# Four 32-row blocks in four column tiles: the within-chunk matrices of an S5 layer inside a four-layer decoder trunk

## The chip, the cores and the metric

One core of one Trainium2 chip runs the whole trunk in one launch. The metric is the device time of that launch in microseconds, the median of the runs. Engines are named as the profile names them: PE (TensorE matmul), PEld (its weight load), DVE (VectorE), ACT (ScalarE), POOL (GpSimd), and SP, the queue that issues most DMAs.

## The reference

Four layers on 256 tokens of width 1024, all in float32. Layers 0 and 3 mix tokens with a gated linear recurrence (HGRN2), layer 1 with an mLSTM, layer 2 with a complex diagonal state space (S5); each is followed by a SwiGLU block of hidden width 2816 and by layer norms. The change concerns S5 alone, of whose parameters the kernel makes matrices:

```python
abar = exp((a_re + i*a_im) * dt)                  # 64 groups x 64 states
bbar = (abar - 1) / a * (b_re + i*b_im)           # 64 x 64 x 16 channels
state[t] = abar * state[t-1] + bbar @ u[t]        # per group, complex
y[t] = real(c @ state[t]) + d_skip * u[t]         # c: 64 x 16 x 64
```

The kernel takes four tokens at a time. Inside such a chunk of four, the output at step j + k depends on the input at step j through real(c · abar^k · bbar) with k = 0 to 3, and for k = 0 the skip d is added. These four 16 x 16 matrices per group are the "matrices within a chunk".

## The kernel before

**Layout.** PE works in float32r with every operand split in a high and a low part (`hi`, `lo` of weights, `xh`, `xl` of tokens), so each product is three matmuls (`mm3`, L137, whose matmuls are L140 to L142). In the blocks of the SwiGLU called `across` (L297) the weights are the stationary side and `ws_wide` (L165) issues L170 (512 columns: high and low tokens at once) and L173 (256 columns). Its result stands in a PSUM bank of tag `g`, of which there are two; ACT copies one half out (L304), DVE adds the other (L305), and only then is the bank free for the next but one call of `ws_wide`. ACT casts each weight tile to `hi` (L123), DVE makes `lo` (L124).

**S5's matrices are made early.** `s5_prepare` (L801) returns two lists of small functions, `spans`. They are called one by one from `fill` (L262) between the pieces of the SwiGLU blocks of layer 0 and of layer 1, so their instructions stand among the matmuls of these two stages on every engine; their products go to DRAM and come back in layer 2. `scalars0` to `table_out` make powers of abar and a table; then for each of four quarters q (8 pairs of groups, a pair filling 128 partitions) come `products_b` (L934), `products_bj` (L948), `products_c` (L963), `turn` (L979, PE transposes) and, for e = 0, 1, `within(q, e)` (L990). Temporaries are tiles `t0` (two buffers) and `t1` (one).

**`within` before.** It runs eight times. For each of four pairs x it multiplies the block `bz[..., 3]` (bbar, 128 rows by 32 columns, real and imaginary part in turn) as stationary side with two moving tiles: c itself, 16 columns, from `bc` (L997), and c times three powers, 48 columns, from `cu` (L999). All 16 matmuls write PSUM partitions 0 to 31 of one bank of tag `t`, 64 columns for each x. These are float32 matmuls, which the trace records as two passes each. Then DVE multiplies the bank with `par` (L1003), adds d (L1005), and ACT copies the result three times to lower partitions (L1007); SP stores it (L1008).

**Order.** Each engine executes in order. The order on an engine is set by the tile framework's scheduler from the code and the free buffers, so a changed buffer can move instructions of other lines too.

Of the kernel before, what the change touches and what calls it, by code (L numbers as in the profile page):

```python
# [9 lines left out]
F32 = mybir.dt.float32  # L10
# [4 lines left out]
ALU = mybir.AluOpType  # L15
AX = mybir.AxisListType

P = 128
# [16 lines left out]
class Trunk:  # L35
# [765 lines left out]
    def s5_prepare(self):  # L801


        nc, a = self.nc, self.a
        mk = lambda name, shape: [self.dram.tile(shape, F32, name=f"{name}{b}") for b in range(8)]
        self.s5_b, self.s5_ct, self.s5_cs = mk("s5b", [P, 2, 512]), mk("s5ct", [P, 3, 512]), mk("s5cs", [P, 2, 256])
        c = self.s5const
# [2 lines left out]
        pb = c.tile([P, 2, 3, 32], F32, name="s5pb")  # L810
        co = c.tile([P, 2, 32], F32, name="s5co")
        dd = c.tile([32, 32], F32, name="s5dd")
        par = c.tile([32, 2, 16], F32, name="s5par")
        tt, ts, stt = nc.vector.tensor_tensor, nc.vector.tensor_scalar, nc.vector.scalar_tensor_tensor
        tile_ = lambda tag, shape, **kw: self.s5pool.tile(shape, F32, tag=tag, name=self.uid(tag), **kw)
        k = {}
# [9 lines left out]
        def temps(*shape):  # L826
            n = int(np.prod(shape))
            dims = "abcd"[: len(shape)]
            out = []
            for tag, bufs in (("t0", 2), ("t1", 1)):  # L830
                t = tile_(tag, [P, 1024], bufs=bufs)[:, :n]
                kw = dict(zip(dims, shape))
                out.append(t.rearrange(f"p ({' '.join(dims)}) -> p {' '.join(dims)}", **kw))
            return out

        def squares(x, y):

            t0, t1 = temps(2, pw[:, 0, x, :].shape[1], 32)
            n = t0.shape[2]
            bc = lambda i: pw[:, i, x, :][:, None].broadcast_to([P, 2, n, 32])  # L840
            cmul(pw[:, :, x, :], bc(0), bc(1), t0, t1, pw[:, 0, y, :], pw[:, 1, y, :])
# [47 lines left out]
        def scalars2():  # L889
            squares(slice(0, 5, 4), slice(1, 6, 4))  # L890
            squares(slice(5, 6), slice(6, 7))
            t0, t1 = temps(2, 2, 32)
            bc = lambda i: pw[:, i, 1:2, :][:, None].broadcast_to([P, 2, 2, 32])
            cmul(pw[:, :, 0:2, :], bc(0), bc(1), t0, t1, pw[:, 0, 2:4, :], pw[:, 1, 2:4, :])
            for j in range(3):
                nc.scalar.copy(pb[:, 0, j, :], pw[:, 0, 2 - j, :])
                nc.scalar.mul(pb[:, 1, j, :], pw[:, 1, 2 - j, :], -1.0)
# [10 lines left out]
        def table_double(n):  # L908
            cs, w = k["cs"], k["w"][:, :, 0:16]
            t0, t1 = temps(2, 16, n)  # L910
            bc = lambda i: w[:, i, None, :, None].broadcast_to([P, 2, 16, n])
            cmul(cs[:, :, :, 0:n], bc(0), bc(1), t0, t1, cs[:, 0, :, n : 2 * n], cs[:, 1, :, n : 2 * n])
            if n < 32:
                w2 = tile_("wn", [P, 2, 32], bufs=2)[:, :, 0:16]
                t0, t1 = temps(2, 16)
                bw = lambda i: w[:, i, None, :].broadcast_to([P, 2, 16])
                cmul(w, bw(0), bw(1), t0, t1, w2[:, 0], w2[:, 1])
                k["w"] = w2
# [43 lines left out]

        def products_c(q):  # L963
            f = slice(8 * q, 8 * q + 8)
            cu, t1 = temps(2, 4, 8, 16)
            k["cu"] = cu
            for i in range(2):
                p = lambda r: pw[:, r, 0:4, f][:, :, :, None].broadcast_to([P, 4, 8, 16])
                x = k["bc"][:, 2 + i : 3 + i].broadcast_to([P, 4, 8, 16])
                tt(cu[:, i], x, p(0), ALU.mult)  # L970
                tt(t1[:, i], x, p(1), ALU.mult)
            tt(cu[:, 0], cu[:, 0], t1[:, 1], ALU.subtract)
            tt(cu[:, 1], cu[:, 1], t1[:, 0], ALU.add)
            for i in range(2):
                for g in range(2):
                    r = slice(64 * g, 64 * g + 64)
                    nc.scalar.copy(k["cz"][r, i, :, :, g, :], cu[r, i].rearrange("p j f c -> p f j c"))
# [12 lines left out]
        def within(q, e):  # L990
            b = 2 * q + e
            ps = self.bank("t")
            for x in range(4):
                f, o = 4 * e + x, ps[0:32, x * 64 : (x + 1) * 64]
                w = lambda i: k["bz"][:, i, f, 3].rearrange("p g c -> p (g c)")
                for i in range(2):
                    nc.tensor.matmul(o[:, 0:16], w(i), k["bc"][:, 2 + i, f], start=i == 0, stop=i == 1)  # L997
                for i in range(2):
                    nc.tensor.matmul(o[:, 16:64].rearrange("p (k c) -> p k c", k=3), w(i), k["cu"][:, i, 0:3, f], start=i == 0, stop=i == 1)  # L999
            tm = k["tm"]  # L1000
            dg = tile_("dg", [32, 4, 32])
            tt(dg, self.ident[0:32, None, 0:32].broadcast_to([32, 4, 32]), dd[:, 4 * b : 4 * b + 4, None].broadcast_to([32, 4, 32]), ALU.mult)
            tt(tm[0:32].rearrange("p f (k g c) -> p (f k) g c", g=2, c=16), ps[0:32, 0:256].rearrange("p (n c) -> p n c", c=16)[:, :, None].broadcast_to([32, 16, 2, 16]),  # L1003
               par[:, None].broadcast_to([32, 16, 2, 16]), ALU.mult)
            tt(tm[0:32, :, 0:32], tm[0:32, :, 0:32], dg, ALU.add)  # L1005
            for j in range(1, 4):
                nc.scalar.copy(tm[32 * j : 32 * j + 32, :, 32 * j : P], tm[0:32, :, 0 : P - 32 * j])  # L1007
            nc.sync.dma_start(self.s5_ct[b][:, 2, :], tm.rearrange("p f k -> p (f k)"))  # L1008
# [4 lines left out]
        for s in range(2):  # L1013
            spans[s].append(pads)
            for q in (2 * s, 2 * s + 1):
                spans[s] += [lambda f=f, q=q: f(q) for f in (products_b, products_bj, products_c)]
                for e in range(2):
                    spans[s] += [lambda q=q, e=e, i=i: turn(q, e, i) for i in range(2)] + [lambda q=q, e=e: within(q, e)]
# [250 lines left out]
def consts():  # L1269
    s, c = np.arange(P)[:, None], np.arange(64)[None, :]  # L1270
    lvl = []
    for m in MASKED:
        t = (c // m) * 2 * m + c % m
        same = s // (2 * m) == t // (2 * m)
        lvl.append(np.concatenate([same & ((s // m) % 2 == h) for h in (0, 0, 1, 1)], 1))
    t = np.arange(P)[None, :]
    return {
        "c_ident": np.eye(P, dtype=np.float32),
        "c_par": np.repeat(np.eye(2, dtype=np.float32), 16, 0)[:, :, None].repeat(16, 2),
        "c_lvl": np.stack(lvl, 1).astype(np.float32),  # L1280
        "c_caus": np.where(s > t, np.float32(BIG), np.float32(0.0)),
    }


def layout(i):
# [7 lines left out]
    for g in range(2):  # L1293
# [29 lines left out]
        "w_so": cols_as(so),  # L1323
    })
    out.update(consts())
    return {k: np.ascontiguousarray(v) for k, v in out.items()}

# [13 lines left out]
```

## Time and profile before

| | us |
|---|---|
| runs (3) | 1303.48, 1305.18, 1306.48; median 1305.18 |
| the profiled execution, its own time | 1304.51 |
| its span in the trace | 1302.6 |
| PE busy | 1278.9 (98%) |
| DVE busy | 965.8 (74%) |
| ACT busy | 709.5 (54%) |

The span is cut in the page into 40 slices of 32.6 us with the busy tenths of each engine; the chain of work that ended last is followed back from the last instruction. The calls of `within` start at 252.0, 271.1, 307.1 and 326.2 us (in the SwiGLU block of layer 0) and at 564.1, 583.1, 618.8 and 637.9 us (layer 1). In the timeline, instructions of one line that follow each other are merged: "x4" is four passes, and the second number is from the start of the first to the end of the last.

### The profile page before, as it was taken

What the parts mean: (1) busy time and instruction counts of PE and PEld (TensorE: products, weight loads), DVE (VectorE), ACT (ScalarE), POOL (GpSimd) and SP (SyncE); (2) the same over time, 40 slices, a digit from 0 to 9 for tenths busy, and PEclk for the clock granted to TensorE, in tenths of its full rate; (3) what the DMA queues carried; (4) which work ended last, traced back from release to release, by engine and by line L of the source; (5) the groups of instructions that cost most, each with busy time, mean ns of one, the idle gap of its engine ahead of it and who ended that gap; (6) DMA issues with size and microseconds to landing.
All of it is one profiled execution on the core that took longest, in us unless ns stands there. A gap on an engine that the chain in (4) does not pass through costs nothing.

```text
span 1302.6 us, 18792 instructions
## 1 busy us (share of the span) xinstructions
PE 1278.9 (98%) x7206; PEld 1077.1 (83%) x7206; DVE 965.8 (74%) x1664; ACT 709.5 (54%) x1130; POOL 52.3 (4%) x75
## 2 busy tenths in 40 slices
PE   8999999999999999999998999999999999999997
PEld 6987788888788888888877778888879878888885
DVE  5888789686687699768489877666585886766664
ACT  6755475665466555657442355555458554455550
POOL 0000200000100110000010000000010001000001
PEclk9999999999999999999999999999999999999999
DMA  8833365756374257756567647555555323755540
GB/s 319 289 130 109 127 249 205 258 188 241 117 259 162 97 205 253 237 197 235 183 242 265 237 147 258 178 192 194 194 182 197 134 98 118 267 194 183 182 153 32
DMA packets 46314, 251.00 MB, mean 193 GB/s; under 512 B 5345, under 2 KB 9457, under 8 KB 19857
## 3 DMA queue, kind: packets, MB, share of 16 engines
q1 hardware_dynamic: 45712, 248.08, 53.5%
q0 software_dynamic: 512, 1.73, 0.4%
q8 instruction: 56, 0.92, 0.3%
q14 instruction: 34, 0.27, 0.1%
HBM read 236.16 MB, written 13.63 MB: 192 GB/s over the span
## 4 chain that ended last, share of the span: by engine, by line
PE 91%; DVE 5%; ACT 2%; issue 1%; DMA 1%; POOL 0%; POOLq 0%; SPq 0%; DVEq 0%; ACTq 0%
PE g L170 18%; PE g L140 10%; PE g L142 9%; PE g L141 9%; PE g L173 9%; PE a L140 8%; PE a L141 8%; PE a L142 8%; PE a L594 1%; PE t L1091 1%; DVE lo L124 1%; PE t L225 1%; PE g L1079 1%; DVE att L598 1%; PE t L982 1%
## 5 line engine op out<-in xcount | busy, mean ns | idle before, releaser
L124 DVE TENSOR_TENSOR lo<-w,hi 128x1024 fp32r<-128x1024 f32 (+1 forms) x394 | 476.9, 1219 | 141.2 <-ACT hi L123 132.5
L123 ACT CAST hi<-w 128x1024 fp32r<-128x1024 f32 (+1 forms) x394 | 411.3, 1049 | 191.1 <-PE a L141 110.5
L170 PE MATMUL g<-xx,hi 128*128 128x512 f32 x1024 | 358.3, 395 | 0.0
L173 PE MATMUL g<-xx,lo 128*128 128x256 f32 x1024 | 267.4, 281 | 0.0
L170 PEld LDWEIGHTS g<-xx,hi 128*128 128x128 f32 x1024 | 186.6, 188 | 34.2
L173 PEld LDWEIGHTS g<-xx,lo 128*128 128x128 f32 x1024 | 192.4, 188 | 10.5
L140 PE MATMUL g<-hi,xx 128*128 128x512 f32 x424 | 172.3, 408 | 5.0 <-ACT hi L123 2.4
L141 PE MATMUL g<-hi,xx 128*128 128x512 f32 x424 | 169.8, 401 | 0.0
L142 PE MATMUL g<-lo,xx 128*128 128x512 f32 x424 | 169.2, 401 | 0.0
L140 PE MATMUL a<-hi,hh 128*128 128x512 f32 x344 | 135.8, 397 | 0.0
L141 PE MATMUL a<-hi,hl 128*128 128x512 f32 x344 | 135.7, 395 | 0.0
L142 PE MATMUL a<-lo,hh 128*128 128x512 f32 x344 | 135.4, 394 | 0.0
L304 ACT COPY sum<-g 128x256 f32<-128x256 f32 x128 | 47.7, 373 | 147.2 <-PE g L170 146.9
L305 DVE TENSOR_TENSOR sum<-g,sum 128x256 f32<-128x256 f32 x128 | 54.3, 424 | 72.2 <-ACT sum L304 71.9
L140 PEld LDWEIGHTS g<-hi,xx 128*128 128x128 f32 x424 | 80.1, 189 | 23.7 <-ACT xx L244 3.9
L142 PEld LDWEIGHTS g<-lo,xx 128*128 128x128 f32 x424 | 80.3, 189 | 17.9 <-DVE lo L124 0.9
L141 PEld LDWEIGHTS g<-hi,xx 128*128 128x128 f32 x424 | 80.4, 190 | 15.4 <-issue 0.2
L141 PEld LDWEIGHTS a<-hi,hl 128*128 128x128 f32 x344 | 64.8, 188 | 14.9 <-DVE hl L294 0.5
L142 PEld LDWEIGHTS a<-lo,hh 128*128 128x128 f32 x344 | 64.7, 188 | 14.9
L140 PEld LDWEIGHTS a<-hi,hh 128*128 128x128 f32 x344 | 64.4, 188 | 13.6 <-ACT hh L293 0.6
L140 PE MATMUL g<-xx,hi 128*128 128x256 f32 x200 | 56.5, 283 | 0.0
L141 PE MATMUL g<-xx,lo 128*128 128x256 f32 x200 | 56.4, 282 | 0.0
(299 smaller groups left out, 1845.0 us busy)
## 6 DMA issues: line engine op xcount, KB each, us to landing
w<-in_w_gu SPq DMA_DIRECT2D x88, 1024.0 KB, 5.0
w<-in_w_dn SPq DMA_DIRECT2D x44, 1024.0 KB, 5.0
w<-in_w_hg SPq DMA_DIRECT2D x30, 1024.0 KB, 5.1
w<-in_w_ml SPq DMA_DIRECT2D x12, 1024.0 KB, 5.0
gb<-in_ln SPq DMA_DIRECT2D x8, 1024.0 KB, 5.0
w<-in_w_ho SPq DMA_DIRECT2D x8, 1024.0 KB, 5.0
w<-in_w_so SPq DMA_DIRECT2D x8, 1024.0 KB, 6.3
ct<-s5ct SPq DMA_DIRECT2D x8, 768.0 KB, 9.5
```

What stands on the lines that cost most here:

```text
L123: nc.scalar.copy(hi[:, c], part[:, c])
L124: nc.vector.tensor_tensor(lo[:, c], part[:, c], hi[:, c].bitcast(F32), ALU.subtract)
L140: mm(ps, lh, rh, start=start, stop=False)
L141: mm(ps, ll, rh, start=False, stop=False)
L142: mm(ps, lh, rl, start=False, stop=stop)
L170: whole = lambda: mm(ps, hi[:, c], self.xx[:, k].rearrange("p i t -> p (i t)"), start=k == 0, stop=k == KD - 1)
L173: mm(ps[:, S:], lo[:, c], self.xh[:, k], start=False, stop=False)
L225: nc.tensor.transpose(pt[:, (k % 4) * P : (k % 4 + 1) * P], z[:, k * P : (k + 1) * P], self.ident)
L304: nc.scalar.copy(t, ps[:, S:])
L305: nc.vector.tensor_tensor(t, ps[:, 0:S], t, ALU.add)
L594: nc.tensor.matmul(pl.rearrange("p (h a t) -> p a h t", h=2, a=2)[:, i], kk[:, i * P : (i + 1) * P], view(q, i * P + m, (256 - m, 2), (2 * ...
L598: nc.vector.copy_predicated(queries(att, m), three(i32(msk[:, MASKED.index(m)])), three(pl))
```

## The change

`products_c` now makes a tile `cu` of five slots, of which slot 0 is c, copied by ACT from `bc`, and slots 1 to 4 are the products with the powers. In `within` one matmul of 64 columns takes slots 0 to 3, so there are 8 matmuls for 16. The block of pair x is written to PSUM partitions 32x to 32x + 31, all four to the same 64 columns of the bank, so the four stationary blocks lie in four column tiles of PE; the loop over real and imaginary part is outside the loop over x. DVE reads the four partition groups one by one, with `par` repeated in each. The temporary `t0` has one buffer now.

```diff
-        par = c.tile([32, 2, 16], F32, name="s5par")
+        par = c.tile([P, 2, 16], F32, name="s5par")
...
-            for tag, bufs in (("t0", 2), ("t1", 1)):
+            for tag, bufs in (("t0", 1), ("t1", 1)):
...
-            cu, t1 = temps(2, 4, 8, 16)
-            k["cu"] = cu
+            k["cu"] = tile_("cu", [P, 2, 5, 8, 16])
+            cu, t1 = k["cu"][:, :, 1:], temps(2, 4, 8, 16)[1]
+            nc.scalar.copy(k["cu"][:, :, 0], k["bc"][:, 2:4])
...
-            for x in range(4):
-                f, o = 4 * e + x, ps[0:32, x * 64 : (x + 1) * 64]
-                w = lambda i: k["bz"][:, i, f, 3].rearrange("p g c -> p (g c)")
-                for i in range(2):
-                    nc.tensor.matmul(o[:, 0:16], w(i), k["bc"][:, 2 + i, f], start=i == 0, stop=i == 1)
-                for i in range(2):
-                    nc.tensor.matmul(o[:, 16:64].rearrange("p (k c) -> p k c", k=3), w(i), k["cu"][:, i, 0:3, f], start=i == 0, stop=i == 1)
+            rows = lambda x: slice(32 * x, 32 * x + 32)
+            for i in range(2):
+                for x in range(4):
+                    f = 4 * e + x
+                    nc.tensor.matmul(ps[rows(x), 0:64].rearrange("p (k c) -> p k c", k=4), k["bz"][:, i, f, 3].rearrange("p g c -> p (g c)"),
+                                     k["cu"][:, i, 0:4, f], start=i == 0, stop=i == 1)
...
-            tt(tm[0:32].rearrange("p f (k g c) -> p (f k) g c", g=2, c=16), ps[0:32, 0:256].rearrange("p (n c) -> p n c", c=16)[:, :, None].broadcast_to([32, 16, 2, 16]),
-               par[:, None].broadcast_to([32, 16, 2, 16]), ALU.mult)
+            for x in range(4):
+                tt(tm[0:32, x].rearrange("p (k g c) -> p k g c", g=2, c=16), ps[rows(x), 0:64].rearrange("p (k c) -> p k c", c=16)[:, :, None].broadcast_to([32, 4, 2, 16]),
+                   par[rows(x), None].broadcast_to([32, 4, 2, 16]), ALU.mult)
```

In the changed kernel lines from the copy on stand one to two lines lower: L967 is the new copy of c, L998 the matmul, L1004 the four DVE products, L1006 the sum with d, L1008 ACT's three copies.

**On PE**, at the first call of `within` (layer 0, q = 0, e = 0), before:

```order
L142 MATMUL a_1609<-lo_2459,hh_2392 128x512
L997 MATMUL t_2606<-bc_2286,big_2260 32x16 x2
L999 MATMUL t_2606<-t_2430,big_2260 32x48 x2
L997 MATMUL t_2606<-bc_2286,big_2260 32x16 x2
L999 MATMUL t_2606<-t_2430,big_2260 32x48 x2
L997 MATMUL t_2606<-bc_2286,big_2260 32x16 x2
L999 MATMUL t_2606<-t_2430,big_2260 32x48 x2
L997 MATMUL t_2606<-bc_2286,big_2260 32x16 x2
L999 MATMUL t_2606<-t_2430,big_2260 32x48 x2
L982 MATMUL t_2651<-ident,big_2260 128x128 x4
```

and now:

```order
L142 MATMUL a_1609<-lo_2461,hh_2392 128x512
L998 MATMUL t_2608<-cu_2430,big_2260 32x64 x8
L983 MATMUL t_2648<-ident,big_2260 128x128 x4
L170 MATMUL g_2657<-xx,hi_2576 128x512
L173 MATMUL g_2657<-xx,lo_2577 128x256 x2
```

Sixteen matmuls became eight in the same place, and this is so at all eight calls.

**On ACT**, at the second call (q = 0, e = 1; `big` is the tile `bz`, `tm` what `within` stores, `sum` and `g` belong to the SwiGLU), before:

```order
L123 CAST hi_2956<-w_2950 128x1024
L1007 COPY tm_2262<-tm_2262 32x4x96
L1007 COPY tm_2262<-tm_2262 32x4x64
L1007 COPY tm_2262<-tm_2262 32x4x32
L304 COPY sum_2865<-g_2848 128x256
L123 CAST hi_2998<-w_2996 128x1024
L90 ACTIVATE sum_2865<-sum_2865 128x256
L304 COPY sum_2885<-g_2868 128x256
```

and now:

```order
L123 CAST hi_2948<-w_2942 128x1024
L961 COPY big_2260<-t_2834 64x32x16 x4
L967 COPY cu_2976<-bc_2832 128x2x128
L1008 COPY tm_2262<-tm_2262 32x4x96
L1008 COPY tm_2262<-tm_2262 32x4x64
L1008 COPY tm_2262<-tm_2262 32x4x32
L304 COPY sum_2857<-g_2840 128x256
L123 CAST hi_2992<-w_2990 128x1024
```

The four copies of the next quarter's `bz` (L961) and the new copy of c now stand ahead of the release of a `g` bank. In the SwiGLU of layer 1 the same place has the same order.

**On ACT**, in the layer norm ahead of the SwiGLU of layer 0 (L244 casts the transposed tokens `xx`), now:

```order
L90 ACTIVATE sg_1655<-g_1630 128x256
L244 CAST xx<-t_1541 128x2x128 x2
L244 CAST xx<-t_1554 128x2x128
L967 COPY cu_2430<-bc_2286 128x2x128
L244 CAST xx<-t_1554 128x2x128
L854 ACT_TABLE_LOAD
```

Before, the two L244 of `t_1554` stood next to each other; now the first quarter's copy of c, which needs the DMA of `bc`, stands between them.

## Rows read from the trace of the kernel before

**Rows 1.** The page: busy time of each engine with its share of the span and number of instructions; the granted TensorE clock in 40 slices (tenths); the shares of the chain that ended last.

```profile
PE 1278.9 (98%) x7206; PEld 1077.1 (83%) x7206; DVE 965.8 (74%) x1664; ACT 709.5 (54%) x1130; POOL 52.3 (4%) x75
PEclk9999999999999999999999999999999999999999
PE 91%; DVE 5%; ACT 2%; issue 1%; DMA 1%; POOL 0%; POOLq 0%; SPq 0%; DVEq 0%; ACTq 0%
```

**Rows 2.** Busy time of each engine in stretches of 20 us: one where the tables are made, then those with the calls of `within`. Columns: stretch and its length; PE, PEld, DVE, ACT, POOL with the number of instructions; granted clock; DMA share; GB/s.

```profile
200.00:220.00 20.00, 20.00 (x108) 17.06 (x107) 19.93 (x46) 9.90 (x15) 1.81 (x1) 1.00 0.55 189
240.00:260.00 20.00, 20.00 (x136) 17.05 (x135) 11.98 (x18) 11.40 (x21) 0.00 (x0) 1.00 0.70 250
260.00:280.00 20.00, 20.00 (x132) 16.95 (x131) 14.56 (x27) 11.78 (x20) 0.00 (x0) 1.00 0.59 200
...
580.00:600.00 20.00, 20.00 (x129) 16.97 (x129) 16.91 (x33) 14.53 (x25) 0.00 (x0) 1.00 0.47 163
```

**Rows 3.** All passes of the two matmul lines of `within`: count, duration of one (ns, min/median/max), first and last start, form.

```profile
L997 PE MATMUL t<-bc,big x128: 179/183/203, 252.0 to 638.9; 128*32 128x16 f32 x128
L999 PE MATMUL t<-t,big x128: 206/206/209, 252.1 to 639.0; 128*32 128x48 f32 x128
```

**Rows 4.** The timeline of PE around the first call (start us, length us, engine, line, operation, passes).

```profile
251.40 0.39 PE L141 MATMUL a<-hi,hl 128*128 128x512 f32 x1
251.63 0.40 PE L142 MATMUL a<-lo,hh 128*128 128x512 f32 x1
251.96 0.30 PE L997 MATMUL t<-bc,big 128*32 128x16 f32 x4
252.11 0.34 PE L999 MATMUL t<-t,big 128*32 128x48 f32 x4
252.28 0.27 PE L997 MATMUL t<-bc,big 128*32 128x16 f32 x4
...
253.00 0.34 PE L999 MATMUL t<-t,big 128*32 128x48 f32 x4
253.27 0.66 PE L982 MATMUL t<-ident,big 128*128 128x128 f32 x4
```

**Rows 5.** The same view, four float32 transposes of 128 columns among the SwiGLU's matmuls, and the duration of one.

```profile
259.37 0.60 PE L982 MATMUL t<-ident,big 128*128 128x128 f32 x4
...
L982 PE MATMUL t<-ident,big x64: 270/272/330, 234.2 to 626.6; 128*128 128x128 f32 x64
```

**Rows 6.** The outputs of layer 2 (L1091), float32 matmuls of 128 columns on stationary blocks of 64 columns, written alternately to PSUM partitions 0 to 63 and 64 to 127 of one bank: a part of their timeline, and the number of their passes in a stretch of 2.15 us.

```profile
697.97 0.27 PE L1091 MATMUL t<-ct,s5u 128*64 128x128 f32 x1
697.97 0.59 PE L1091 MATMUL t<-ct,s5hs 128*64 128x128 f32 x6
698.30 0.27 PE L1091 MATMUL t<-ct,s5u 128*64 128x128 f32 x1
...
697.70:699.85 2.15, 2.15 (x40) 2.04 (x38) 1.00 0.83 237
```

**Rows 7.** DVE's instructions of `within` and one of the SwiGLU's reads of a `g` bank (page row: busy us, mean ns).

```profile
L1003 DVE TENSOR_TENSOR tm<-t,s5par x8: 670/672/672, 254.1 to 640.0; 32x512 f32<-32x512 f32 x8
L1005 DVE TENSOR_TENSOR tm<-tm,dg x8: 278/280/281, 254.8 to 640.7; 32x128 f32<-32x128 f32 x8
L305 DVE TENSOR_TENSOR sum<-g,sum 128x256 f32<-128x256 f32 x128 | 54.3, 424 | 72.2 <-ACT sum L304 71.9
```

**Rows 8.** Timeline of ACT, DVE and PE after the second call of `within`.

```profile
270.97 1.04 ACT L123 CAST hi<-w 128x1024 fp32r<-128x1024 f32 x1 [1.75 <-PE a L141]
274.26 1.26 ACT L1007 COPY tm<-tm 32x384 f32<-32x384 f32 x3 [2.24 <-DVE tm L1005]
275.58 0.37 ACT L304 COPY sum<-g 128x256 f32<-128x256 f32 x1
...
279.59 1.31 ACT L961 COPY big<-t 64x512 f32<-64x512 f32 x2
...
272.05 1.23 DVE L124 TENSOR_TENSOR lo<-w,hi 128x1024 fp32r<-128x1024 f32 x1 [1.57 <-ACT hi L123]
276.68 0.42 DVE L305 TENSOR_TENSOR sum<-g,sum 128x256 f32<-128x256 f32 x1
...
272.41 0.50 PE L170 MATMUL g<-xx,hi 128*128 128x512 f32 x1
277.89 0.63 PE L170 MATMUL g<-xx,hi 128*128 128x512 f32 x2
```

**Rows 9.** Timeline of DVE and PE in the stretch where the tables are made.

```profile
203.17 0.69 DVE L821 TENSOR_TENSOR t<-big,wn 128x512 f32<-128x512 f32 x1
206.80 0.42 DVE L305 TENSOR_TENSOR sum<-g,sum 128x256 f32<-128x256 f32 x1
...
208.72 0.62 PE L170 MATMUL g<-xx,hi 128*128 128x512 f32 x2
```

**Rows 10.** The first DMA of `bc` and ACT's casts of the layer norm near it (timeline), and the time to landing of the four DMAs of `bc`.

```profile
158.14 0.67 SPq L937 DMA_DIRECT2D bc<-in_s_bc  x1
...
162.88 0.82 ACT L244 CAST xx<-t 128x256 fp32r<-128x256 f32 x2 [1.24 <-DVE x L221]
164.94 0.37 ACT L244 CAST xx<-t 128x256 fp32r<-128x256 f32 x1 [1.23 <-PE t L225]
...
DMA to landing us min/median/max: 3.0/4.1/5.3
```

More of the change, by code (lines that the diff above doesn't have):

```diff
@@ L1278, in consts @@
         "c_ident": np.eye(P, dtype=np.float32),
-        "c_par": np.repeat(np.eye(2, dtype=np.float32), 16, 0)[:, :, None].repeat(16, 2),
+        "c_par": np.tile(np.repeat(np.eye(2, dtype=np.float32), 16, 0), (4, 1))[:, :, None].repeat(16, 2),
         "c_lvl": np.stack(lvl, 1).astype(np.float32),
```

## The prediction

> **What bounds the kernel now.** I read the engines' totals first: PE is busy for 98% of the span at full granted clock, and the chain that ended last lies on PE for 91% [rows 1]. Totals are averages, so the next view is the stretches that hold the calls of `within`: there PE is busy for 20.00 of 20.00 us each time, DVE for 12 to 17, ACT for 11 to 15 [rows 2]. A matmul removed here lets every later one start earlier; a DVE or ACT instruction added here costs nothing as long as it doesn't make PE wait. The exception is the stretch from 200 to 220 us, where DVE is busy for 19.93 us [rows 2]; there an instruction added on DVE must be looked at.
>
> **PE, removed.** A call of `within` has 16 passes of 16 columns and 16 of 48 (128 each in eight calls [rows 3]). The duration of one pass, some 0.2 us, is mostly pipeline and overlaps with the next one. What counts is the step from start to start: length of a merged group, less one duration, over the passes less one. For L997 (0.27 - 0.18) / 3 = 0.03 us, for L999 (0.34 - 0.206) / 3 = 0.045 us [rows 3, 4]. Sixteen of each make 1.2 us. From the first pass to the next other matmul it is 253.27 - 251.96 = 1.31 us; that includes the last step, 0.14 us from the last pass to L982 (the last of the four L999 starts 3 x 0.045 us after 253.00) [rows 4]. Ahead of the first pass stand 0.33 us where two ordinary matmuls are 0.23 us apart [rows 4], so entering the narrow form costs 0.10 us. Entry and exit stay, since the new matmuls also use 32 columns of weights.
>
> **PE, added.** Eight matmuls of 64 columns are 16 passes. No row has this shape, so its step is bounded by neighbours. If passes follow each other as they do in one column tile, the step grows with the columns: 0.045 us at 48, and (0.60 - 0.27) / 3 = 0.11 us at 128 [rows 5]; 64 columns lie near 0.056 us, 16 passes take 0.90 us. That is one end. For the other, look at the outputs of layer 2: 128 columns too, but alternating between two column tiles. There 40 passes started in 2.15 us, 0.054 us each [rows 6], half of the 0.11 us that a pass of 128 columns takes in one tile. Two column tiles of one PSUM bank thus overlap here, in float32 and with all 128 rows in use. The timeline shows how: passes stand in pairs (697.97 and 697.97, then 698.30) [rows 6]. I read a pair as the second pass of one matmul beside the first of the next, since the two passes of a matmul must use the same tile. By that reading four tiles don't overlap more than two, and a matmul, two passes, costs what one pass costs alone. The new shape is this one with both sizes halved (32 columns of weights for 64, 64 moving for 128), so I take one matmul at 0.056 us, eight at 0.45 us, and the exit at 0.15 us: 0.60 us. This neighbour is nearer than the row of one tile, for it changes tiles as the new code does.
>
> Saved per call: 1.31 - 0.60 = 0.71 us, less 0.01 us for a first step that is somewhat longer with more columns: 0.70 us. Eight calls: **5.6 us**. All eight stand where PE is full [rows 2], and nothing that PE does next waits for the stored matrices before layer 2, so I count all of it on the path. Ends kept for the range: 2.5 us (0.90 us of passes and 0.10 to 0.15 us of exit, saving 0.31 per call) and 8 us (all four tiles at once, so that 16 passes take little over 0.15 us).
>
> The Trainium skill speaks against the overlap: "TensorE: Matmul & The Clock Gate", in the section on packing small matmuls by row and column tiling, says that a weight load overlaps with running matmuls only where the row group differs; all four blocks here use all rows. By that rule the sum would be the 2.5 us. The trace does not agree: the outputs of layer 2 use all rows too, and their passes start 0.054 us apart against 0.11 us in one tile [rows 5, 6].
>
> **DVE.** The product with `par` was one instruction of 512 columns at 0.67 us, and is four of 128 columns. The nearest row is the sum with d, 128 columns on the same 32 partitions, at 0.28 us [rows 7]; that reading PSUM is no dearer is seen from L305, whose 256 columns from PSUM take 0.42 us [rows 7], between the two. So four take at most 1.12 us, 0.45 more per call, 3.6 us in all. At the first call DVE has 8 us of idle time in 20 [rows 2]: nothing on the path.
>
> **ACT.** Four copies of c, 256 columns each, at the 0.37 us of L304's copy of that size [rows 8]: 1.5 us, hidden in the same way. Order matters more. After the second call (and the same place in layer 1) four L961 and the copy of c now precede the copies of `tm` and the L304 that frees a `g` bank. The cast L123 ends at 272.0 us before; a saving of 0.7 at the first call makes it 271.3. Four L961 at 1.31 / 2 us at most are 2.6 us, to 273.9; the copy of c to 274.3; L1008's three copies, 1.26 us as before, to 275.5; L304 to 275.9, L305 to 276.3 [rows 8]. PE wants this bank after two calls of `ws_wide`. Before, its first L170 came at 272.41, and the next but one is the second L170 of the group at 277.89, about 278.1; now both are 1.4 us earlier, 276.7 us [rows 8]. Some 0.4 us are left where 1.0 was (278.1 less 277.10, the end of L305 at 276.68): no stall, cost nothing; without that cover it would be the missing part, tenths of a us at two places.
>
> **The buffer.** With one `t0` and a tile of its own for `cu`, the scheduler places two products with powers (512 columns, 0.69 us each as L821 [rows 9]) among the tables of layer 0, where DVE is full. They delay what follows by up to 1.4 us until DVE catches up. There the bank freed at 207.22 (L305) is wanted about 208.94, the second L170 of the group at 208.72 [rows 9]: 1.7 us of slack. Nothing.
>
> **The new wait.** The first copy of c waits for the DMA of `bc`, issued at 158.14 and landing 3.0 to 5.3 us later, at 163.4 at the latest, 164.1 if counted from the end of issue [rows 10]. It stands ahead of the last L244 of the layer norm, which starts at 164.94; the one ahead ends at 163.70 [rows 10]. The copy fits between, to 164.5. Behind it on ACT are that cast, a table load and the next weights' casts; PE waits for the cast. SP has no new step ahead of these.
>
> **The sum.** 1304.51 - 5.6 = 1298.9 us for the profiled execution. The median of the runs stands 0.67 us above it, so I forecast **1299.6 us**. 0.2%, 2.6 us, is about what a measurement of this kernel can tell from no change.
>
> **The rivals.**
> - *No overlap*: the passes follow each other at 0.056 us. Saved 2.5 us: 1302.7 us, within 0.2%. For it: the duration of the passes grows with the columns [rows 4, 5]; against it, the pairs of L1091 [rows 6]. 13%.
> - *Four tiles at once*: 8 us saved, 1297.2 us. Against it: the pairs are never groups of three, but only two tiles were in use there. 6%.
> - *DVE or ACT in front*: the overlap is there, but a `g` bank comes late at two to four places, by about 1 us each, as the slacks of 0.4 and 1.7 us could allow if the new order is worse than I added up. 1 to 4 us are given back: 1300.6 to 1303.6 us. 10%.
> - *Each change of tile drains the array*, and this is the one that ends slower. Entering the narrow form costs 0.10 us [rows 4]. If each of the seven changes of tile in a call cost the same, a call would take 0.90 + 0.70 + 0.15 = 1.75 us against 1.31, and 8 x 0.44 = 3.5 us would be lost: 1308.7 us. It decides from about 0.04 us per change on ((1.31 - 1.05) / 7). Against it: the outputs of layer 2 change tile at every matmul and pay nothing [rows 6]; for it: that had two tiles of 64, not four of 32. 6%.
>
> **How the numbers follow.** My forecast has 65%, the rivals 13, 6, 10 and 6%. Faster by over 0.2% are the forecast, four tiles and most of the late banks: 0.77. Within 0.2%: no overlap, which is on the edge, and the rest: 0.16. Slower: the drain, and a stall not thought of: 0.07. The range leaves out the drain and most of what lies beyond: from 1296.8 (four tiles, a little below) to 1303.4 us (no overlap with a small stall).
>
> **What would show it.** In the changed kernel L998 should have 128 passes of 64 columns, a call should take about 0.6 us from its first pass to the next other matmul, with a pass started every 0.028 us on the mean; one every 0.056 us means no overlap, 0.1 us a drain. L1004 should show 0.28 us. PE should stay at 20.00 of 20.00 us in these stretches; a gap ahead of an L170 that ended by DVE's L305 would show a late bank, a longer gap around 164 us a late copy of c. If the calls shrink as said and the time does not, the prediction is wrong in that PE's time counts in full.

## The result and the profile after

The changed kernel takes 1296.41 us (median of 6 runs, 1295.68 to 1298.58), the kernel before 1305.15 us (6 runs, 1303.48 to 1306.48): 8.74 us less between the two medians. The ratio estimated from all the runs, which is not that of the two medians, is 0.9939 with a 95% interval of 0.9928 to 0.9951; it stands for 8.0 us, and the ratios below are of the same kind. The forecast was 1299.6 us with 5.6 us saved; the direction was right, the size was not, and the median lies just under the low end of the range, 1296.8 us. The profiled execution took 1295.68 us, its span 1293.8 us.

The page has the same shape as before [rows 1]: PE busy for 98% of the span, its granted clock at 0.9 or more in every slice, and the chain that ended last on PE for 91%. The other shares of the chain are those of before within one percent of the span.

```profile
PE 1270.1 (98%) x7078; PEld 1068.1 (83%) x7078; DVE 968.7 (75%) x1688; ACT 709.6 (55%) x1134; POOL 52.4 (4%) x75
PEclk9999999999999999999999999999999999999999
PE 91%; DVE 4%; ACT 2%; issue 1%; DMA 1%; POOL 0%; SPq 0%; POOLq 0%; DVEq 0%; ACTq 0%
```

The stretch where the tables are made and three with the calls, columns as in [rows 2]. PE is still busy for 20.00 of 20.00 us, so neither a late `g` bank nor a late copy has opened a gap:

```profile
200.00:220.00 20.00, 20.00 (x107) 17.08 (x106) 19.79 (x45) 10.00 (x15) 0.00 (x0) 1.00 0.55 196
240.00:260.00 20.00, 20.00 (x126) 16.90 (x125) 15.90 (x28) 12.12 (x21) 0.00 (x0) 1.00 0.77 275
260.00:280.00 20.00, 20.00 (x121) 16.80 (x120) 14.45 (x25) 14.95 (x28) 0.00 (x0) 1.00 0.57 200
580.00:600.00 20.00, 20.00 (x110) 17.22 (x110) 14.64 (x24) 15.67 (x29) 0.44 (x6) 1.00 0.70 243
```

The timeline of PE at the first call answers to [rows 4]; under it the instructions of the new lines (count, duration ns min/median/max, first and last start):

```profile
251.65 0.39 PE L141 MATMUL a<-hi,hl 128*128 128x512 f32 x1
251.88 0.40 PE L142 MATMUL a<-lo,hh 128*128 128x512 f32 x1
252.21 0.43 PE L998 MATMUL t<-cu,big 128*32 128x64 f32 x16
252.57 0.66 PE L983 MATMUL t<-ident,big 128*128 128x128 f32 x4
```

```profile
L998 PE MATMUL t<-cu,big x128: 219/219/244, 252.2 to 631.7; 128*32 128x64 f32 x128
...
L1004 DVE TENSOR_TENSOR tm<-t,s5par x32: 278/284/292, 252.7 to 632.9; 32x128 f32<-32x128 f32 x32
...
L967 ACT COPY cu<-bc x4: 398/407/409, 163.9 to 582.0; 128x256 f32<-128x256 f32 x4
```

From the first pass to the next other matmul it is 252.57 - 252.21 = 0.36 us, where it was 1.31 us and 0.60 was forecast. All sixteen passes lie in one merged group of 0.43 us, of which one pass alone is 0.22. The entry ahead of it is unchanged (252.21 - 251.88 = 0.33 us, 0.10 more than between two ordinary matmuls). Summed over the eight calls, from the trace's single records (one for each pass, with its start in ns), the stretch from first pass to next matmul fell from 10.44 to 2.89 us: **7.55 us** of the difference of 8.83 between the two profiled executions (1304.51 - 1295.68).

The single records show how. These are the starts of the 16 passes of the first call, in ns from the first one, for this kernel and for three of the experiments below:

```
change, four tiles      0   6  13  20 |  80  86  93 100 | 135 142 149 155 | 191 198 205 211
e3, pair outer          0  14  27  40 |  80  94 109 120 | 136 150 165 176 | 192 205 220 232
e4, two tiles           0   7 |  80  87 | 136 143 | 192 199 | 248 254 | 304 310 | 359 366 | 415 422
e1, one tile            0 |  80 | 136 | 192 | 247 | 303 | 359 | 415 | 471 | 527 | 582 | 638 | 694 | 750 | 806 | 862
```

In the change the passes come in four rounds of four, 6 to 7 ns apart within a round. The rounds start at 0, 80, 135 and 191 ns; in one tile the first four passes start at 0, 80, 136 and 192. I read this so: each column tile goes through its own four passes as if it were alone, and all four tiles do so at once. The experiments test that reading.

### The profile page after: what moved, and what is told of

Its sections match the earlier page's. It is cut to its first block, busy times and chain, and to the rows that moved or that the text cites. A ratio compares the mean times of both kernels' runs of the same rounds, so it can differ in the third digit from the quotient of the medians.

```text
span 1293.8 us, 18572 instructions
## 1 busy us (share of the span) xinstructions
PE 1270.1 (98%) x7078; PEld 1068.1 (83%) x7078; DVE 968.7 (75%) x1688; ACT 709.6 (55%) x1134; POOL 52.4 (4%) x75
## 4 chain that ended last, share of the span: by engine, by line
PE 91%; DVE 4%; ACT 2%; issue 1%; DMA 1%; POOL 0%; SPq 0%; POOLq 0%; DVEq 0%; ACTq 0%
PE g L170 18%; PE g L140 10%; PE g L141 10%; PE g L142 10%; PE g L173 9%; PE a L140 8%; PE a L141 8%; PE a L142 8%; PE a L594 2%; PE t L1092 1%; PE t L225 1%; DVE lo L124 1%; PE g L1080 1%; DMA xt<-in_xt 1%; PE t L983 1%
## 5 line engine op out<-in xcount | busy, mean ns | idle before, releaser
L170 PE MATMUL g<-xx,hi 128*128 128x512 f32 x1024 | 358.3, 395 | 0.0
L170 PEld LDWEIGHTS g<-xx,hi 128*128 128x128 f32 x1024 | 186.7, 188 | 34.4
L304 ACT COPY sum<-g 128x256 f32<-128x256 f32 x128 | 47.6, 372 | 142.2 <-PE g L170 142.0
L305 DVE TENSOR_TENSOR sum<-g,sum 128x256 f32<-128x256 f32 x128 | 54.2, 423 | 67.0 <-ACT sum L304 66.5
```

The costliest lines, as they stand in the source:

```text
L170: whole = lambda: mm(ps, hi[:, c], self.xx[:, k].rearrange("p i t -> p (i t)"), start=k == 0, stop=k == KD - 1)
L304: nc.scalar.copy(t, ps[:, S:])
L305: nc.vector.tensor_tensor(t, ps[:, 0:S], t, ALU.add)
```

## Experiments

Three theories stood against each other. **A**: each column tile takes its own passes in turn, and the tiles run side by side. **B**: passes start in order, and one that waits for its tile holds up those behind it, so that only neighbours in the order overlap. **C**: most of the gain comes from the merge into 64 columns, not from the tiles. Where nothing else is said an experiment is the changed kernel with one edit. Each time is the median of five or more runs beside runs of the kernel before on the same chip: that one took 1304.78 us (1303.47 to 1306.95) beside e1 to e4, and 1305.33 (1301.51 to 1307.18) beside e5 to e8. The durations of calls are the mean of eight, from the first pass to the next other matmul.

### e1: the merge alone

```diff
-            for i in range(2):
-                for x in range(4):
-                    f = 4 * e + x
-                    nc.tensor.matmul(ps[rows(x), 0:64]...
+            for x in range(4):
+                f = 4 * e + x
+                for i in range(2):
+                    nc.tensor.matmul(ps[0:32, 64 * x : 64 * x + 64]...
...
-            for x in range(4):
-                tt(tm[0:32, x]..., ps[rows(x), 0:64]...)
+            tt(tm[0:32]..., ps[0:32, 0:256]..., par[0:32, None]..., ALU.mult)
```

> The change with one part undone: c and its products stay in one tile and one matmul of 64 columns, but all four blocks are written to partitions 0 to 31 (one column tile), and DVE reads them with one instruction as in the kernel before. Theory A (each column tile takes its own passes in turn, so tiles run side by side): nothing overlaps here, 15 steps of 0.056 us and an exit of 0.15 us, 1.0 us per call against 0.36 in the change; the time is the change's plus 8 x 0.63 = 5.0 us, near 1301.4, some 3 us under the kernel before. Theory B (passes overlap only with their neighbour in program order, whatever the tile): the same. Rival C (most of the gain is the merge into 64 columns, not the tiles): near 1297.

1301.33 us (1298.65 to 1302.13), ratio 0.9968 [0.9956, 0.9981]. PE's timeline at the first call:

```profile
249.77 1.08 PE L997 MATMUL t<-cu,big 128*32 128x64 f32 x16
250.78 0.65 PE L983 MATMUL t<-ident,big 128*128 128x128 f32 x4
```

A call takes 1.01 us; behind the first step of 80 ns the passes start 56 ns apart, as worked out ahead of the result from the 48 and 128 columns. The merge gives 0.29 of the 0.94 us. C falls.

### e2: the tiles alone

```diff
-            for i in range(2):
-                for x in range(4):
-                    ...
-                    nc.tensor.matmul(ps[rows(x), 0:64]..., k["cu"][:, i, 0:4, f], ...)
+            for lo, hi in ((0, 1), (1, 4)):
+                for i in range(2):
+                    for x in range(4):
+                        ...
+                        nc.tensor.matmul(ps[rows(x), 16 * lo : 16 * hi]..., k["cu"][:, i, lo:hi, f], ...)
```

> The other part undone: four column tiles, but c (16 columns) and its products (48 columns) are multiplied by separate matmuls, 16 in a call. Theory A: four rounds of four passes at about 0.031 us and four at 0.043 us, 0.26 us and an exit of 0.14: 0.40 to 0.45 us per call, the change's time plus 0.3 to 0.7 us, near 1297. Theory B (only neighbours in the order overlap, two at a time): half of the 32 steps of the kernel before, 0.6 us and the exit, 0.75 us per call, near 1299.5. Rival C: near 1303.

1296.12 us (1294.82 to 1296.84), ratio 0.9932 [0.9919, 0.9944]. The 32 passes form one group:

```profile
251.87 0.50 PE L999 MATMUL t<-cu,big 128*32 128x16 f32 x32
252.31 0.44 PE L983 MATMUL t<-ident,big 128*128 128x128 f32 x2
```

A call takes 0.435 us, 0.07 more than in the change. Once the tiles run side by side, the merge is worth 8 x 0.07 = 0.6 us; the time doesn't show so little. A holds, C falls a second time.

### e3: both parts of one pair in a row

```diff
-            for i in range(2):
-                for x in range(4):
+            for x in range(4):
+                for i in range(2):
```

> The change with the two loops of the matmuls swapped: for each block x first the real and then the imaginary part, so four passes of one column tile follow each other in program order before the next tile's. Theory A (a pass waits only for its own tile, later ones of other tiles go past it): still rounds of four passes, 0.36 us per call, 1296.4 us. Theory B (in order: a pass that waits for its tile holds up all behind it): 12 steps of 0.056 us and three short ones, 0.7 us, with the exit 0.85 us per call, 8 x 0.49 = 3.9 us more than the change, near 1300.3.

1297.76 us (1296.80 to 1300.23), ratio 0.9947 [0.9933, 0.9960].

```profile
252.57 0.45 PE L998 MATMUL t<-cu,big 128*32 128x64 f32 x16
252.95 0.66 PE L983 MATMUL t<-ident,big 128*128 128x128 f32 x4
```

Here four passes of one tile follow each other in the program before the next tile has any. A call takes 0.381 us, not the 0.85 of B: the passes still start in four rounds (list above), now some 13 ns apart in a round, about 7 ns for each matmul ahead in the program. A waiting pass doesn't hold up another tile's. The records don't say which tile a pass belongs to; that a round is one pass of each tile is read from the steps. Read in program order instead, a round would be the four passes of one tile, 13 ns apart; against that stands e1, where passes of one tile never start closer than 55 ns. The time is 1.3 us over A's 1296.4, while the calls take only 0.16 us more in sum; its interval overlaps the change's, and the rest lies in layer 2, as is shown below.

### e4: two column tiles

```diff
-            rows = lambda x: slice(32 * x, 32 * x + 32)
-            for i in range(2):
-                for x in range(4):
-                    f = 4 * e + x
+            rows = lambda x: slice(32 * (x % 2), 32 * (x % 2) + 32)
+            cols = lambda x: slice(64 * (x // 2), 64 * (x // 2) + 64)
+            for h in range(2):
+                for i in range(2):
+                    for x in (2 * h, 2 * h + 1):
+                        f = 4 * e + x
...
+                        nc.tensor.matmul(ps[rows(x), cols(x)]...
```

> The change with two column tiles for four: blocks 0 and 2 in the first, 1 and 3 in the second, at other columns. Both theories: pairs of passes, 7 to 8 steps of 0.056 us and an exit of 0.15, 0.54 to 0.60 us per call, 8 x 0.2 = 1.6 us more than the change, near 1298; this is the size that was forecast for four tiles. If four tiles bring nothing over two, the time is the change's.

1299.28 us (1297.81 to 1299.51), ratio 0.9954 [0.9942, 0.9967].

```profile
252.31 0.64 PE L1000 MATMUL t<-cu,big 128*32 128x64 f32 x16
252.89 0.66 PE L983 MATMUL t<-ident,big 128*128 128x128 f32 x4
```

A call takes 0.572 us, with pairs 56 ns apart: twice one tile's rate, and nearly the 0.60 us that was forecast for four tiles. The three sizes line up: first to last pass 0.862 us with one tile, 0.422 with two, 0.211 with four. The median is 2.9 us over that of the change where 1.6 were expected and the calls give 1.68; the remainder, too, is taken up below.

### e5: the old matmuls in the new surroundings

The eight calls explain 7.55 us of 8.83. Could the reordering by the buffers have given the rest?

```diff
-                    nc.tensor.matmul(ps[rows(x), 0:64]..., k["cu"][:, i, 0:4, f], ...)
+                for i in range(2):
+                    nc.tensor.matmul(o[:, 0:16], w(i), k["cu"][:, i, 0, f], ...)
+                for i in range(2):
+                    nc.tensor.matmul(o[:, 16:64]..., w(i), k["cu"][:, i, 1:4, f], ...)
...
-            for x in range(4):
-                tt(tm[0:32, x]..., ps[rows(x), 0:64]...)
+            tt(tm[0:32]..., ps[0:32, 0:256]..., par[0:32, None]..., ALU.mult)
```

> The change with the matmuls of `within` and its DVE product as they were before (16 and 48 columns, one column tile, one DVE instruction of 512 columns); the tile cu with its copy of c, the single t0 and par stay as in the change. It asks where the part of the change's gain lies that the eight calls don't show: the calls became 7.55 us shorter, the profiled run 8.8. If the remainder of 1.2 us is the reordering by the buffers, this kernel is about 1.2 us faster than the one before: 1303.6 us. If the remainder is the half-clock stretch of layer 2, which is longer in one profile than in another without any edit of it, the times of this kernel and of the one before are the same within their spread: 1304.8 us. In both cases a call takes 1.31 us.

1305.16 us (11 runs, 1303.33 to 1307.14), ratio 1.0002 [0.9993, 1.0011]; a call takes 1.305 us. The tile `cu`, the copies of c and the single `t0` by themselves change nothing that can be measured; a gain of 1.2 us would be a ratio of 0.9991, just below the interval.

### e6: the temporary with two buffers

```diff
-            for tag, bufs in (("t0", 1), ("t1", 1)):
+            for tag, bufs in (("t0", 2), ("t1", 1)):
```

> The change with t0 at two buffers again, as before: PE's order is that of the change, only DVE's order differs. My prediction costs the two delayed products with powers at nothing. If that holds, the time is that of the change, 1296.4 us; if they make a g bank late, this kernel is faster than the change by up to 1.4 us, 1295.0.

1296.28 us (1295.43 to 1299.26), ratio 0.9941 [0.9927, 0.9955], the same as the change beside it (e8). The products delayed on DVE cost nothing that these runs can show.

### e7: both calls of a quarter together

```diff
-                    spans[s] += [...turn...] + [lambda q=q, e=e: within(q, e)]
+                    spans[s] += [...turn...]
+                spans[s] += [lambda q=q: (within(q, 0), within(q, 1)), lambda: None]
```

> The change with the two calls of a quarter (e = 0 and 1) made one after the other at the place of the second, so that 16 matmuls stand in a row four times. With four tiles at once a call in the change takes 0.36 us, 0.15 of it exit, behind an entry that is 0.10 us longer than between ordinary matmuls; of each pair of calls one entry and one exit go, and the rounds of four (0.056 us each) run on: 0.21 + 0.06 + 0.21 + 0.15 = 0.6 us from the first pass to the next matmul, for 0.72 and a second entry of 0.10. About 0.2 us four times: 1295.6 us, 0.8 less than the change, if ACT and DVE, which get both calls' copies at once, don't make a g bank late; if they do at two places by about 0.5 us each, 1296.6.

1294.85 us (1293.97 to 1297.79), ratio 0.9929 [0.9916, 0.9942].

```profile
258.73 0.65 PE L998 MATMUL t<-cu,big 128*32 128x64 f32 x32
259.31 0.50 PE L170 MATMUL g<-xx,hi 128*128 128x512 f32 x1
259.65 0.40 PE L173 MATMUL g<-xx,lo 128*128 128x256 f32 x2
```

The edit puts both calls one place ahead of the second call's: the first pair starts at 258.73 us, where the second call of e8 starts at 270.52. Thirty-two passes take 0.584 us to the next matmul, eight rounds without a break between the calls; two calls of the change take 0.72 and have two entries. From the second matmul behind the last call on, PE's matmuls start 1.28 us earlier than in the profile of e8 (631.12 against 632.40 us), 0.07 of which were there before the first call: 1.2 us, more than the 0.8 expected. The expectation left out a part of the exit. The first full-width matmul behind a call is followed by the next one only 259.65 - 259.31 = 0.34 us later, where 0.23 is ordinary, and this too falls away with each place that is saved. PE waits for no `g` bank in this profile. This is the fastest median of all; its interval overlaps that of e8, so that it beats the change is shown in the trace and not by the medians.

### e8: the change once more

> The change once more, unedited, on the chip of these runs, to set the others against and to see a second profile of it. Calls of 0.36 us, 2.9 us in all, and a total of 1296.4 us, 1295.7 to 1298.6. If the half-clock stretch in layer 2 is one of the run and not of the kernel, it stands at another place or is of another length than in the first profile of the change (where it began in the stretch from 703.5 to 708.6 us).

1297.22 us (1296.03 to 1298.63), ratio 0.9942 [0.9929, 0.9954]; calls of 0.361 us, 2.89 in sum. Against the kernel before on its own chip the change saves 0.0058 x 1305.33 = 7.6 us here and 0.0061 x 1305.15 = 8.0 us in the first comparison; the intervals, 6.0 to 9.4 us over the two, hold the 7.55 of the calls.

### What is left beside the calls

For each profiled execution, the sum of the eight calls is taken off its own time:

| | own time | calls | rest |
|---|---|---|---|
| before | 1304.51 | 10.44 | 1294.07 |
| e5, old matmuls, new surroundings | 1303.51 | 10.44 | 1293.07 |
| e1, one tile | 1299.89 | 8.09 | 1291.80 |
| e4, two tiles | 1299.28 | 4.57 | 1294.71 |
| e2, not merged | 1296.14 | 3.48 | 1292.66 |
| e3, pair outer | 1298.07 | 3.05 | 1295.02 |
| change | 1295.68 | 2.89 | 1292.79 |
| e8, change again | 1296.56 | 2.89 | 1293.67 |
| e6, two buffers | 1295.43 | 2.89 | 1292.54 |
| e7, calls together | 1294.85 | 2.34 | 1292.51 |

The rest is 1291.8 to 1295.0 us, and it doesn't follow the calls: the lowest stands beside long calls, the highest beside short ones. The same kernel gives 1292.79 and 1293.67, and the kernels with unchanged calls 1294.07 and 1293.07. The 1.28 us between before and change (8.83 - 7.55) lie within this scatter.

With PE's matmuls outside the calls matched in order, each trace with that of the change, it can be seen where the scatter arises: in the first 60 us and in layer 2 (665 to 760 us). The table has how much later than in the change the matmuls stand by 60 us, what is added in layer 2, and the granted clock from 0 to 40 and from 660 to 760 us:

| | start, us | clock | layer 2, us | clock |
|---|---|---|---|---|
| before | -0.33 | 0.96 | 1.41 | 0.97 |
| e5, old matmuls, new surroundings | -1.60 | 1.00 | 1.86 | 0.97 |
| e1, one tile | -2.45 | 1.00 | 1.45 | 0.97 |
| e4, two tiles | 0.13 | 1.00 | 1.93 | 0.97 |
| e2, not merged | -0.35 | 0.96 | 0.08 | 0.98 |
| e3, pair outer | 0.33 | 0.96 | 1.97 | 0.97 |
| change | 0 | 0.96 | 0 | 0.98 |
| e8, change again | 0.11 | 1.00 | 0.43 | 0.98 |
| e6, two buffers | -1.62 | 1.00 | 1.36 | 0.97 |
| e7, calls together | 0.06 | 0.96 | 0.17 | 0.98 |

From 60 to 665 us the calls account for all of the difference but 0.12 us or less (before: 7.67 us, of which 7.55 in the calls; e7 apart, whose entries and exits stand outside the calls' durations), and behind 760 us at most 0.16 us are added. So what is taken off the calls comes off the end in full, and the rest comes from two stretches without a call. In layer 2 it goes with the clock: the profiles at 0.97 lose 1.36 to 1.97 us against the change, those at 0.98 at most 0.43. At the start it goes with the clock only in part: e1, e5 and e6 are early at 1.00, but e4 and e8 at 1.00 are not.

PE's granted clock falls from 2.4 to 1.2 GHz for short stretches, at the start of the program and in layer 2, where PE waits for DVE. In the rows below the columns are those of [rows 2], the granted clock third from the end; before, the change, and the change again (e8):

```profile
0.00:40.00 40.00, 36.42 (x214) 30.03 (x215) 24.71 (x27) 27.00 (x36) 2.58 (x9) 0.96 0.85 315
660.00:760.00 100.00, 94.04 (x597) 76.99 (x598) 83.02 (x137) 33.37 (x45) 1.71 (x2) 0.97 0.65 242
```

```profile
0.00:40.00 40.00, 36.52 (x211) 29.45 (x212) 24.38 (x26) 26.67 (x35) 2.61 (x9) 0.96 0.84 313
660.00:760.00 100.00, 94.30 (x603) 76.89 (x602) 82.39 (x136) 33.98 (x43) 3.38 (x4) 0.98 0.65 240
```

```profile
0.00:40.00 40.00, 36.96 (x210) 30.29 (x211) 24.26 (x26) 26.55 (x35) 2.61 (x9) 1.00 0.83 310
660.00:760.00 100.00, 93.91 (x601) 76.47 (x600) 81.99 (x135) 33.14 (x42) 3.42 (x4) 0.98 0.66 241
```

The change has 0.96 in its first 40 us in one profile and 1.00 in the other, with no edit between them. In layer 2 its low stretch begins in 703.5 to 708.6 us in one and ends soon after (first fence), and lies mostly in 688.9 to 692.6 us in the other (second fence):

```profile
703.50:708.60 5.10, 2.91 (x27) 2.80 (x28) 5.07 (x11) 0.00 (x0) 0.00 (x0) 0.71 0.71 253
708.60:712.00 3.40, 3.40 (x41) 3.23 (x38) 3.37 (x7) 1.93 (x3) 0.00 (x0) 0.93 0.71 214
```

```profile
684.00:688.90 4.90, 4.04 (x29) 3.19 (x28) 3.52 (x7) 1.09 (x2) 0.00 (x0) 1.00 0.62 220
688.90:692.60 3.70, 2.41 (x24) 2.44 (x26) 3.70 (x8) 1.20 (x2) 0.00 (x0) 0.60 0.84 260
```

In the profile of before the low clock went on after PE was full again: the second row below has PE busy for 4.00 of 4.00 us at 0.58, where the change, in the second row of its fence, has 0.93.

```profile
711.00:716.00 5.00, 2.81 (x28) 2.70 (x29) 4.96 (x11) 0.00 (x0) 0.00 (x0) 0.65 0.76 281
716.00:720.00 4.00, 4.00 (x32) 3.67 (x30) 3.51 (x7) 1.86 (x3) 0.00 (x0) 0.58 0.53 166
```

In before this part loses 1.41 us against the change, and its start is 0.33 us ahead: with the calls and the 0.12 us between, 8.75 of the 8.83 us. So the step from 7.55 to 8.83 us is put down to the longer low stretch. No edit tested the clock itself, but e5 speaks against the new surroundings (between 60 and 665 us it differs from before by 0.13 us), and in e8 the stretch moved by itself. What makes one profile lose more of the clock than another, and what else moves the start by up to 2.8 us, stays open.

The mean granted clock of each run tells the same. Four of the change's six runs have 0.996 and took 1295.68 to 1296.62 us; the other two have 0.994 and 0.993 and took 1298.12 and 1298.58. In a straight-line fit to the 76 runs with a clock, one level for each kernel on each chip and one slope for all, 0.001 of clock goes with 0.78 us. At the same clock of 0.996 the fit gives 1304.2 and 1304.3 us for before, 1296.2 for the change, 1296.5 for e8, 1296.6 for e3 and 1295.1 for e7, each give or take 0.2 to 0.4: an estimate of 8 us for the change, not clear of the calls' 7.55, and 1.2 to 1.4 more for the calls together.

## Why the prediction was right in direction and wrong in size

**What bounds the kernel: held.** PE was full where the calls stand, and what was taken from them came off the end (table above): calls shorter in sum by 5.87, 7.39 and 7.55 us (e4, e3, the change) gave ratios that stand for 4.3 to 7.6, 5.2 to 8.7 and 6.4 to 9.4 us. For e1 and e2, with calls shorter by 2.35 and 6.96 us, the lower ends are 2.5 and 7.3 us: there a little more came than the calls show, and the profiles have it at the start (e1) and in layer 2 (e2). What the 8.74 us between the medians hold beyond the calls' 7.55 is not shown to be the kernel's; the prediction had no term for what the clock does in layer 2, and that this went in the change's favour here was luck.

**The step that failed** is the one put as "four tiles don't overlap more than two, and a matmul, two passes, costs what one pass costs alone". It gave 8 x 0.056 = 0.45 us for the passes of a call, 0.60 us with the exit and 5.6 us in all. Measured were 0.211 us, 0.361 us and 7.55 us. The exit was right (0.150 us from the last pass to L983, 0.15 forecast), the entry too, and the step of a pass in one tile as well (56 ns, in e1). The fault lay in what [rows 6] can tell. The outputs of layer 2 alternate between two tiles only. There "each tile by itself, all at once" and "a pass beside its neighbour in the order" give the same 0.054 us and the same pairs; e4 shows that with two tiles the forecast 0.60 us is nearly met (0.572). The row was right and couldn't decide the case of four tiles. The text said as much among the rivals ("only two tiles were in use there") and yet left *Four tiles at once* 6%. That rival was the case: its 8 us and 1297.2 us stand against 7.55 us and 1296.41.

**The rule weighed against the trace.** The Trainium skill's "TensorE: Matmul & The Clock Gate", in the section on packing small matmuls, lets a weight load overlap running matmuls only where the row group differs. All blocks here use all 128 rows, and by that rule the change and e1 would take the same time per call; they took 0.36 and 1.01 us. The measurement decides against the rule for this shape. The same page's section "Why this matters for your kernels" gives 2.38 times the speed for three column tiles of 32 columns with 512 moving columns; no run here has that shape, but its direction is what the runs show: from first to last pass 0.862 / 0.211 = 4.1 times for four tiles and 64 columns.

**DVE: held.** L1004 takes 0.284 us (0.28 forecast from the sum with d), four of them 1.18 us in the timeline below, 0.06 over the bound. DVE rose to 15.90 of 20 us at the first call, and PE stayed at 20.00.

**ACT's order and the second bank: held, with less to spare.** The same stretch as [rows 8], ACT, DVE and PE (in brackets the engine's idle time before it, and what ended it):

```profile
270.27 1.05 ACT L123 CAST hi<-w 128x1024 fp32r<-128x1024 f32 x1 [1.75 <-PE a L141]
271.22 2.51 ACT L961 COPY big<-t 64x512 f32<-64x512 f32 x4
273.74 0.41 ACT L967 COPY cu<-bc 128x256 f32<-128x256 f32 x1
274.18 1.26 ACT L1008 COPY tm<-tm 32x384 f32<-32x384 f32 x3
275.46 0.37 ACT L304 COPY sum<-g 128x256 f32<-128x256 f32 x1
...
270.90 1.18 DVE L1004 TENSOR_TENSOR tm<-t,s5par 32x128 f32<-32x128 f32 x4 [1.11 <-PE t L998]
...
275.87 0.42 DVE L305 TENSOR_TENSOR sum<-g,sum 128x256 f32<-128x256 f32 x1 [0.53 <-ACT sum L304]
...
276.23 0.63 PE L170 MATMUL g<-xx,hi 128*128 128x512 f32 x2
```

L304 starts at 275.46 (forecast 275.5) and L305 ends at 276.29 (forecast 276.3). The second L170 of the group comes about 0.23 us after 276.23, at 276.46. So 0.17 us are left where 0.4 were forecast: PE came sooner, since the calls were shorter. *DVE or ACT in front* did not happen, but by these rows a second call shorter by another 0.2 us would have met it here in this order.

**The copy of c behind the DMA: held.** It runs between the two casts, and the second cast waits for PE:

```profile
163.13 0.82 ACT L244 CAST xx<-t 128x256 fp32r<-128x256 f32 x2 [1.25 <-DVE x L221]
163.85 0.41 ACT L967 COPY cu<-bc 128x256 f32<-128x256 f32 x1
165.20 0.38 ACT L244 CAST xx<-t 128x256 fp32r<-128x256 f32 x1 [0.94 <-PE t L225]
```

All of this stretch stands 0.25 us later than in [rows 10], the casts before the copy too, so the copy isn't the cause. It takes 0.41 us, not the 0.37 taken from L304.

**The buffer: held** (e5, e6). **No overlap** and **Each change of tile drains the array** fell: a start every 56 ns in one tile and every 14 ns on the mean in four (0.211 / 15 us), no drain at seven changes of tile.

## What to carry to other kernels

Put small float32 matmuls with 32 columns of weights in four column tiles, at output partitions 0, 32, 64 and 96: here a call's passes then took a quarter of the time, and a matmul that isn't merged costs little more. Put such matmuls in one place: each place cost 0.10 us to enter and 0.15 to leave, the last pass's own step in it, together more than the 0.21 us from the first to the last of sixteen passes, and four places less saved 1.2 us. And when a neighbouring row with two of something is used for a case with four, ask which theories it can't tell apart, and spread the chances over them.

## What the runs showed of the hardware

- Four column tiles, all with 128 rows, run side by side in float32: rounds of four passes 6 to 7 ns apart, the rounds as far apart as passes in one tile (56 ns at 64 columns).
- Passes of one tile don't hold up those of another that stand behind them in the program (e3: 0.381 us, where starting in order would take 0.85).
- The step of a float32 pass with 32 columns of weights in one tile: 31 ns at 16 columns, 43 ns at 48 (before, e5), 56 ns at 64 (e1).
- Behind narrow matmuls the first full-width matmul is followed by the next 0.34 us later, where 0.23 is ordinary (e7).
- The granted clock falls to the lower level in layer 2 at places that change between profiles of one kernel, and a low stretch can outlast the wait ahead of it (4.00 us of full PE at 0.58).
